# A two-layer trunk on one core: mixers' raw weight buffers at the other end of SBUF, FFN tiles in another order, ten unread products in the first projection

## The chip, the cores and the metric

One NeuronCore of one Trainium2 chip runs the whole program. The metric is device time in microseconds of one execution; the number given is the median of three. A profile is one execution recorded by the hardware profiler. TensorE is written PE, VectorE DVE, ScalarE ACT, GpSimd POOL and SyncE SP.

## What is computed

The input x is 512 tokens of 1024 values, fp32. Layer 0 mixes tokens with a gated MLP block and latent attention, layer 1 with retention; each mixer is followed by a SwiGLU FFN with 2816 hidden columns.

```python
def reference(x, ...):
    for l in range(2):
        h = rmsnorm(x, norm_mix[l])
        x = x + (even_mixer(h, ...) if l % 2 == 0 else odd_mixer(h, ...))
        h = rmsnorm(x, norm_ffn[l])
        x = x + swiglu(h, ffn_w_gate[l], ffn_w_up[l], ffn_w_down[l])
    return x

def swiglu(h, w_gate, w_up, w_down):
    return (jax.nn.silu(h @ w_gate) * (h @ w_up)) @ w_down
```

## The kernel before

**Products.** x lies transposed in SBUF as eight tiles of 128 features by 512 tokens. Every fp32 operand of a large product is split into a high and a low part (`split`, L281 to L283: ACT writes the high part, DVE the rest), and a product is three PE products (`mm3`, L288 to L290). `project` multiplies all eight h tiles by one or several weight tiles; `h_tiles` are written by `scaled_parts` (ACT L357, DVE L358).

**Weights.** All weights stand in one list in the order of their use, the tape. `Tape.load` takes the next entry: SP issues the DMA into a raw tile (L211), ACT casts the high part (L214), DVE makes the low part (L215). The parts have four slots, so an entry is cast when the entry four before it has been used up. `tape.ahead()` loads until four entries are ahead. A raw tile is written by the next load of its slot only after ACT and DVE have read it. Raw tiles come from a pool that each stage opens for itself: 3 tiles in the mixers (L429, L992), 7 in the FFNs (L823), 4 KB per partition each. Loads that the end of a stage issues ahead go into that stage's pool: the first four FFN entries lie in the mixer's raw tiles.

**FFN.** Pair 0 of column tiles is multiplied plainly (four entries, "whole"). The others go in pairs by a scheme with seven products in place of eight (L867): entries A11, A12 and A22 are loaded, S1 and S3 are sums of two blocks, for which SP loads the first and POOL adds the second by an accumulating DMA (L213), and S2 and S4 are added by DVE in place (L199). The h side needs sums too: `sums(k)` copies two x tiles to a `J` tile on ACT (L837), makes the four sums on DVE (L846 to L849, four operations) and splits them into `t_hi`, `t_lo`. The code has the first projection, then `ss.columns` (the norm's transposes, L318), `sums(0)`, `sums(1)`, the second projection, `sums(2)`, `sums(3)`, then the products. `finish` writes the activations to `a_hi0` to `a_hi7` and `a_lo0` to `a_lo7`, column tile m to number m % 8; `down` reads them in three parts, pairs 0 to 3, 4 to 7 and 8 to 10.

**Memory.** Pools that live throughout lie lowest. A stage opens its pools one above the other from the same base, in the order of the code, and closes them at its end. Before, each stage's raw pool is the first and so begins at the base. With `reuse_waits="tile"` a new tile waits for the readers and writers of those older tiles that lay at its own bytes, not for the whole pool. Above the base, in KB per partition, the FFN has raw 28, `fp` 64 (`t_hi`, `t_lo` 32, then `a` 32), `fp2` 20 (`J` 16, `t` 4). Layer 1's mixer has raw 12, `tmp` 16 (eight tiles `w`), then `od`: `cs` 4, `decay` 8, small ones, `R_turns`, the parts of q, k and v, attention weights, gates `g0` to `g3`, `Ro` and, last, `y0` to `y3`, the normed and gated head outputs that the output projection multiplies.

**Order.** The tile framework puts each engine's instructions into one queue, at compile time, and sets the waits. Instructions of one engine are not always in the order of the code. At run time an engine takes its queue in order.

**Start.** Twelve products of `ones` by `ones` into the bank `warm` (L276) precede the first projection; nothing reads that bank. x arrives in five chunks of 1, 1, 2, 2 and 2 tiles.

Of the kernel before, what the change touches and what calls it, by code (L numbers as in the profile page):

```python
# [11 lines left out]
F32R = mybir.dt.float32r  # L12
# [4 lines left out]
P = 128  # L17
# [129 lines left out]

CHUNK = 1024


HALF = 256
SHORT = 64
# [2 lines left out]
def turns(m, d):  # L155


    if m.shape[1] == 2 * d:
        return m.rearrange("p (j d) -> p d j", j=2)
    return m.rearrange("p (b j d) -> p b d j", j=2, d=d)  # L160
# [75 lines left out]
def trunk_kernel(ctx: ExitStack, tc: tile.TileContext, a: dict, out: bass.AP):  # L236
    nc = tc.nc
# [9 lines left out]
    def new_tmp(stack, bufs=2):  # L247
        env["tmp"] = stack.enter_context(tc.tile_pool(name="tmp", bufs=bufs, reuse_waits="tile"))
# [4 lines left out]
    def bank(name="bank"):  # L253
        return ps.tile([P, S], F32, name=name, tag="bank")

    tape = Tape(nc, parts, a["wtape"])

    def new_raw(stack, bufs):
        tape.raw = stack.enter_context(tc.tile_pool(name="raw", bufs=bufs, reuse_waits="tile"))

    gains = const.tile([P, 4, KD], F32, name="gains")
    nc.scalar.dma_start(out=gains, in_=a["gains"])
# [4 lines left out]
    ones = const.tile([P, P], F32, name="ones")  # L267
# [6 lines left out]
    warm = bank("warm")  # L274
# [6 lines left out]
    def split(dst_hi, dst_lo, src):  # L281
        nc.scalar.copy(dst_hi, src)  # L282
        nc.vector.tensor_tensor(dst_lo, src, f32(dst_hi), op=ALU.subtract)  # L283

    def mm3(acc, stat, mov, start, stop, d=HALF):

        (sh, sl), (mh, ml) = stat, [turns(m, d) for m in mov]
        nc.tensor.matmul(acc, sh, mh, start=start, stop=False)  # L288
        nc.tensor.matmul(acc, sh, ml, start=False, stop=False)  # L289
        nc.tensor.matmul(acc, sl, mh, start=False, stop=stop)  # L290
# [61 lines left out]
    def scaled_parts(which, k):  # L352


        hi, lo = h_tiles(k)
        g = gains[:, which, k : k + 1]
        nc.scalar.activation(hi, x[k], AF.Identity, scale=g)  # L357
        nc.vector.scalar_tensor_tensor(  # L358
            lo, x[k], g, f32(hi), op0=ALU.mult, op1=ALU.subtract
        )  # L360
        return hi, lo

    def project(h, n=1, name="ps_mm", d=HALF):

        w = [tape.next() for _ in range(n)]
        accs = [bank(name) for _ in range(n)]
        nk = w[0][0].shape[1]
        for k in range(nk):
            for (hi, lo), acc in zip(w, accs):
                mm3(acc, (hi[:, k, :], lo[:, k, :]), h[k], k == 0, k == nk - 1, d)  # L370
        tape.ahead()
        return accs[0] if n == 1 else accs

# [52 lines left out]


    with ExitStack() as e:
        new_raw(e, 3)  # L429
        h = []  # L430
        for k0, k1 in ((0, 1), (1, 2), (2, 4), (4, 6), (6, 8)):
            nc.sync.dma_start(out=x_all[:, k0:k1, :], in_=a["xP"][:, k0:k1, :])
# [45 lines left out]
            latp.append((hi, lo))  # L478

        kv_ss, q_ss = Norm(), Norm()  # L480
        accs = [project(h) for _ in range(3)]
        ss.columns(D)
        rcol = ss.kept_columns(ev)
        accs.append(project(h))
        R = ss.rows(norm)
        for acc in accs[:2]:
            kv_ss.add(latent(acc))
        q_ss.add(latent(accs[2]))
        q_ss.add(latent(accs[3]))
        q_ss.add(latent(project(h)))  # L490

        nc.vector.tensor_tensor(
# [37 lines left out]
        for i in range(NT):  # L530
# [4 lines left out]
                start=True,  # L535
                stop=True,
# [277 lines left out]
    def ffn(h, ss, which):  # L814
# [5 lines left out]


        with ExitStack() as e:
            new_raw(e, 7)  # L823
            fp = e.enter_context(tc.tile_pool(name="fp", bufs=1, reuse_waits="tile"))
            fp2 = e.enter_context(tc.tile_pool(name="fp2", bufs=2, reuse_waits="tile"))
            q = S // 2
            act = {}
            stands = {n: [] for n in ("A11", "A12", "S4", "S1", "S2", "S3", "A22")}
# [1 line left out]
            def wide():  # L830
                return fp2.tile([P, 2 * S], F32, name="J", bufs=4)

            def sums(k):

                f = wide()
                for j in range(2):
                    nc.scalar.activation(  # L837
                        f[:, j * S : (j + 1) * S],
                        x[2 * k + j],
                        AF.Identity,  # L840
                        scale=gains[:, which, 2 * k + j : 2 * k + j + 1],
                    )
                b11, b12, b21, b22 = (f[:, i * q : (i + 1) * q] for i in range(4))
                t = wide()
                t1, t2, t3, t4 = (t[:, i * q : (i + 1) * q] for i in range(4))
                nc.vector.tensor_tensor(t1, b11, b12, op=ALU.subtract)  # L846
                nc.vector.scalar_tensor_tensor(t2, t1, -1.0, b22, op0=ALU.mult, op1=ALU.subtract)
                nc.vector.tensor_tensor(t3, b22, b12, op=ALU.subtract)
                nc.vector.scalar_tensor_tensor(t4, t2, -1.0, b21, op0=ALU.mult, op1=ALU.subtract)  # L849
                hi = fp.tile([P, 4 * q], F32R, name=f"t_hi{k}")  # L850
                lo = fp.tile([P, 4 * q], F32R, name=f"t_lo{k}")
                split(hi, lo, t)
                for i, n in enumerate(("S1", "S2", "S3", "A22")):
                    stands[n].append([v[:, i * q : (i + 1) * q] for v in (hi, lo)])
                for n, j, i in (("A11", 0, 0), ("A12", 1, 0), ("S4", 1, 1)):
                    stands[n].append([v[:, i * q : (i + 1) * q] for v in h[2 * k + j]])
# [74 lines left out]
            for k in range(2):  # L931
                sums(k)
            whole.append(project(h, 2))
            for k in range(2, 4):
                sums(k)
# [45 lines left out]
    h = [scaled_parts(2, k) for k in range(KD)]  # L981
    h2 = []
    ss2 = None
    for k in ffn(h, ss, 2):
        ss2 = ss2 or Norm()
        h2.append(scaled_parts(1, k))
        ss2.add(x[k])
    h, ss = h2, ss2


    with ExitStack() as e:
        new_raw(e, 3)  # L992
        new_tmp(e)
        od = e.enter_context(tc.tile_pool(name="od", bufs=1, reuse_waits="tile"))
        cs = od.tile([P, 2, S], F32, name="cs")
# [5 lines left out]
        def parts_tile(name, n=S):  # L1001
            return (od.tile([P, n], F32R, name=name + "_hi"), od.tile([P, n], F32R, name=name + "_lo"))

        def rotated(name, accs):
            a1, a2 = (undone(acc) for acc in accs)
            c, s = plain(cs[:, 0, :]), plain(cs[:, 1, :])
            o = [tmp([P, S], "w", bufs=8), tmp([P, S], "w", bufs=8)]
            t = [tmp([P, S], "w", bufs=8), tmp([P, S], "w", bufs=8)]
            nc.vector.tensor_tensor(plain(o[0]), a1, c, op=ALU.mult)
            nc.vector.tensor_tensor(plain(t[1]), a1, s, op=ALU.mult)  # L1010
            nc.vector.tensor_tensor(plain(t[0]), a2, s, op=ALU.mult)
            nc.vector.tensor_tensor(plain(o[1]), a2, c, op=ALU.mult)
            nc.vector.tensor_tensor(o[0], o[0], t[0], op=ALU.subtract)
            nc.vector.tensor_tensor(o[1], o[1], t[1], op=ALU.add)
            got = []
            for j in range(2):
                p = parts_tile(f"{name}{j}")
                split(*p, o[j])
                got.append((*p, o[j]))
            return got  # L1020

        prev = None
        for hd in range(RH):
            accs = project(h, 2)
# [3 lines left out]
            else:  # L1028
                so.columns(512)
                q = rotated("q", accs)  # L1030
            accs2 = project(h, 2)
            if hd == 0:
# [5 lines left out]
                q = rotated("q", accs)  # L1038
            else:
                gated()  # L1040
            k = rotated("k", accs2)
            v = []
            for i, acc in enumerate(project_tokens(h, 4, 2)):
# [4 lines left out]
                hi, lo = parts_tile(f"v{i}")  # L1048
# [14 lines left out]
            for j in range(NT - 1):  # L1063
                n = S - j * P
# [62 lines left out]
    for m in ffn(h2, ss, 3):  # L1127
        nc.sync.dma_start(out=out[m * P : (m + 1) * P, :], in_=x[m])
# [69 lines left out]
```

## Time and profile before

| | |
|---|---|
| median of 3 runs | 1235.24 us (1233.83 to 1236.07) |
| the profiled execution | 1235.62 us |
| its span in the trace | 1233.8 us |
| PE busy | 1219.8 us, 99% |
| DVE, ACT, POOL busy | 853.1, 562.7, 83.7 us |
| granted clock over the span | 0.997 |

A busy time counts instructions as they lie in the trace; ends of products are modelled, so PE's busy time contains half-clock stretches and short waits. "Granted clock" is the share of PE's full clock in a stretch: 1.00 is 2.4 GHz, 0.50 is 1.2 GHz. In a timeline the columns are start, duration, engine, line, operation, tiles written and read, count, and in brackets the idle time of the engine before it with what ended it.

### The profile page before, as it was taken

The numbers are of one execution on the slowest core, as the hardware profiler recorded it, in microseconds if no ns is written. First come the engines' busy times: TensorE is split into PE (matmuls) and PEld (weight loads), VectorE is DVE, ScalarE is ACT, GpSimd is POOL, SyncE is SP. The second block draws the span as 40 slices with busy tenths as digits, with TensorE's granted clock in tenths as the row PEclk, the third lists the DMA queues.
The fourth block names the chain that finished last, engine by engine and source line by source line (L and its number), as shares of the span: only waits on it lengthen the run. The fifth ranks groups of instructions, "written<-read, shape, count | busy, mean of one in ns | idle before, by whom it ended". The sixth has DMA issues, their size and how long they took to land. (4 is left out here: it accounts for less than half of the span.)

```text
span 1233.8 us, 18406 instructions
## 1 busy us (share of the span) xinstructions
PE 1219.8 (99%) x7464; PEld 1105.8 (90%) x7464; DVE 853.1 (69%) x1224; ACT 562.7 (46%) x809; POOL 83.7 (7%) x84
## 2 busy tenths in 40 slices
PE   8999999999999999999999999999998999999998
PEld 7897778998999899888888888888888989998997
DVE  6597749875687577955574474574778756876774
ACT  5455747652465255533342242242465623652551
POOL 2072001000000000000000000000010000000000
PEclk9999999999999999999999999999999999999999
DMA  7223007555575466223122332332266555754631
GB/s 238 86 73 116 35 35 205 155 171 148 143 205 163 128 161 194 91 69 115 57 103 69 103 103 69 103 103 69 86 188 157 174 146 142 203 167 123 166 108 69
DMA packets 44772, 155.32 MB, mean 126 GB/s; under 512 B 5376, under 2 KB 5776, under 8 KB 44560
## 3 DMA queue, kind: packets, MB, share of 16 engines
q1 hardware_dynamic: 38304, 131.06, 31.8%
q0 software_dynamic: 6240, 23.08, 10.8%
q8 instruction: 58, 0.95, 0.3%
q14 instruction: 26, 0.21, 0.1%
q10 hardware_dynamic: 144, 0.02, 0.0%
HBM read 152.04 MB, written 2.10 MB: 125 GB/s over the span
## 5 line engine op out<-in xcount | busy, mean ns | idle before, releaser
L214 ACT CAST w_hi<-w_raw 128x1024 fp32r<-128x1024 f32 (+2 forms) x288 | 294.0, 1027 | 477.9 <-PE ps_mm L289 223.0
L215 DVE TENSOR_TENSOR w_lo<-w_raw,w_hi 128x1024 fp32r<-128x1024 f32 (+2 forms) x288 | 345.1, 1205 | 122.7 <-ACT w_hi L214 122.2
L288 PE MATMUL ps_mm<-h_hi,w_hi 128*128 128x512 f32 x456 | 175.6, 385 | 2.1 <-ACT h_hi L357 1.5
L289 PE MATMUL ps_mm<-h_lo,w_hi 128*128 128x512 f32 x456 | 173.8, 382 | 0.8 <-DVE h_lo L358 0.7
L290 PE MATMUL ps_mm<-h_hi,w_lo 128*128 128x512 f32 x456 | 173.5, 381 | 0.0
L867 PE MATMUL ps_x<-t_hi,w_hi 128*128 128x256 f32 x480 | 133.2, 278 | 4.1 <-ACT J L896 4.0
L288 PE MATMUL ps_mm<-a_hi,w_hi 128*128 128x512 f32 x352 | 133.3, 380 | 0.3 <-ACT a_hi L282 0.3
L289 PE MATMUL ps_mm<-a_lo,w_hi 128*128 128x512 f32 x352 | 133.4, 379 | 0.0
L290 PE MATMUL ps_mm<-a_hi,w_lo 128*128 128x512 f32 x352 | 133.4, 379 | 0.0
L867 PE MATMUL ps_x<-t_hi,w_lo 128*128 128x256 f32 x480 | 132.8, 277 | 0.0
L867 PE MATMUL ps_x<-t_lo,w_hi 128*128 128x256 f32 x480 | 132.7, 277 | 0.0
L288 PEld LDWEIGHTS ps_mm<-h_hi,w_hi 128*128 128x128 f32 x456 | 86.6, 190 | 15.7 <-ACT h_hi L357 2.2
L289 PEld LDWEIGHTS ps_mm<-h_lo,w_hi 128*128 128x128 f32 x456 | 86.6, 190 | 13.6 <-DVE h_lo L358 1.8
L290 PEld LDWEIGHTS ps_mm<-h_hi,w_lo 128*128 128x128 f32 x456 | 86.6, 190 | 12.7 <-DVE w_lo L215 0.4
L867 PEld LDWEIGHTS ps_x<-t_hi,w_hi 128*128 128x128 f32 x480 | 92.9, 194 | 5.3 <-ACT J L896 5.3
L867 PEld LDWEIGHTS ps_x<-t_lo,w_hi 128*128 128x128 f32 x480 | 92.9, 194 | 0.0
L867 PEld LDWEIGHTS ps_x<-t_hi,w_lo 128*128 128x128 f32 x480 | 92.9, 193 | 0.0
L213 POOL DMA_DIRECT2D w_raw<-in_wtape x40 | 34.8, 870 | 623.6 <-DVE t L881 159.2
L288 PEld LDWEIGHTS ps_mm<-a_hi,w_hi 128*128 128x128 f32 x352 | 66.4, 189 | 10.3 <-ACT a_hi L282 1.1
L290 PEld LDWEIGHTS ps_mm<-a_hi,w_lo 128*128 128x128 f32 x352 | 66.5, 189 | 9.4
L289 PEld LDWEIGHTS ps_mm<-a_lo,w_hi 128*128 128x128 f32 x352 | 66.6, 189 | 9.2
L925 DVE TENSOR_TENSOR t<-ps_mm,R 128x512 f32<-128x512 f32 x48 | 33.1, 689 | 58.8 <-PE ps_mm L290 58.6
(221 smaller groups left out, 2590.6 us busy)
## 6 DMA issues: line engine op xcount, KB each, us to landing
w_raw<-in_wtape SPq DMA_DIRECT2D x225, 512.0 KB, 3.4
w_raw<-in_wtape POOLq DMA_DIRECT2D x40, 512.0 KB, 6.1
w_raw<-in_wtape SPq DMA_DIRECT2D x19, 384.0 KB, 3.5
out_T<-x SPq DMA_DIRECT2D x8, 256.0 KB, 2.0
x<-in_xP SPq DMA_DIRECT2D x3, 512.0 KB, 7.5
w_raw<-in_wtape SPq DMA_DIRECT2D x4, 256.0 KB, 6.0
decay<-in_decay POOLq DMA_DIRECT2D x1, 1024.0 KB, 7.5
x<-in_xP SPq DMA_DIRECT2D x2, 256.0 KB, 3.6
```

The costliest lines, as they stand in the source:

```text
L213: nc.gpsimd.dma_start(out=t[:, c], in_=more[:, c], accum_op=ALU.add)
L214: nc.scalar.copy(hi[:, c], t[:, c])
L215: nc.vector.tensor_tensor(lo[:, c], t[:, c], hi[:, c].bitcast(F32), op=ALU.subtract)
L288: nc.tensor.matmul(acc, sh, mh, start=start, stop=False)
L289: nc.tensor.matmul(acc, sh, ml, start=False, stop=False)
L290: nc.tensor.matmul(acc, sl, mh, start=False, stop=stop)
L867: nc.tensor.matmul(o, s[:, k, cols], m, start=start and k + f + n == 0, stop=k == KD // 2 - 1 and n == 2, skip_group_check=True,)
L925: nc.vector.tensor_tensor(plain(t), undone(accs[j]), plain(R), op=ALU.mult)
```

## The change

The raw pools of the three stages get a side: `right` for the two mixers, which puts the pool at the upper end of SBUF and lets `tmp` and the pools after it move down by 12 KB, and `left` for the FFNs. The FFN's one pool `fp` is divided: `ft` (`t_hi`, `t_lo`) comes directly above the raw tiles, then `fp2` (`J`, `t`), then `fp` with the `a` tiles alone. The very first projection gets 6, 2, 1 and 1 products of `ones` by `ones` into `warm` in the code behind its first four chunks of products.

```diff
+IDLE = (6, 2, 1, 1)
-    def new_raw(stack, bufs):
-        tape.raw = stack.enter_context(tc.tile_pool(name="raw", bufs=bufs, reuse_waits="tile"))
+    def new_raw(stack, bufs, side):
+        tape.raw = stack.enter_context(tc.tile_pool(name="raw", bufs=bufs, side=side, reuse_waits="tile"))
-    def project(h, n=1, name="ps_mm", d=HALF):
+    def project(h, n=1, name="ps_mm", d=HALF, idle=()):
                 mm3(acc, (hi[:, k, :], lo[:, k, :]), h[k], k == 0, k == nk - 1, d)
+            for _ in range(idle[k] if k < len(idle) else 0):
+                nc.tensor.matmul(warm[:, :P], ones, ones, start=True, stop=True)
         tape.ahead()
-        new_raw(e, 3)
+        new_raw(e, 3, "right")
-        accs = [project(h) for _ in range(3)]
+        accs = [project(h, idle=IDLE), project(h), project(h)]
-            new_raw(e, 7)
+            new_raw(e, 7, "left")
+            ft = e.enter_context(tc.tile_pool(name="ft", bufs=1, reuse_waits="tile"))
+            fp2 = e.enter_context(tc.tile_pool(name="fp2", bufs=2, reuse_waits="tile"))
             fp = e.enter_context(tc.tile_pool(name="fp", bufs=1, reuse_waits="tile"))
-            fp2 = e.enter_context(tc.tile_pool(name="fp2", bufs=2, reuse_waits="tile"))
-                hi = fp.tile([P, 4 * q], F32R, name=f"t_hi{k}")
-                lo = fp.tile([P, 4 * q], F32R, name=f"t_lo{k}")
+                hi = ft.tile([P, 4 * q], F32R, name=f"t_hi{k}")
+                lo = ft.tile([P, 4 * q], F32R, name=f"t_lo{k}")
-        new_raw(e, 3)
+        new_raw(e, 3, "right")
```

## Rows read from the trace of the kernel before

**Rows 1.** The page, engine shares: busy time, share of the span, instructions.

```profile
PE 1219.8 (99%) x7464; PEld 1105.8 (90%) x7464; DVE 853.1 (69%) x1224; ACT 562.7 (46%) x809; POOL 83.7 (7%) x84
```

**Rows 2.** Waits of PE, whole span: what waited, for what, total us, times, longest.

```profile
PE ps_x L867 <- ACT J L896: 4.0, 2, 2.8
```

**Rows 3.** Windows: us, busy by engine (instructions), granted clock, DMA share, GB/s.

```profile
206.75:231.38 24.63, 24.63 (x178) 23.34 (x176) 23.48 (x32) 17.34 (x22) 2.92 (x3) 1.00 0.47 108
907.95:940.01 32.06, 27.32 (x178) 25.27 (x176) 24.35 (x33) 15.59 (x20) 4.61 (x5) 0.95 0.76 201
...
936.00:939.20 3.20, 3.20 (x17) 3.20 (x17) 3.00 (x4) 0.48 (x1) 0.00 (x0) 0.50 0.70 155
```

**Rows 4.** Timeline of ACT, layer 1's FFN start.

```profile
917.49 1.04 ACT L214 CAST w_hi<-w_raw 128x1024 fp32r<-128x1024 f32 x1 [6.50 <-DMA w_raw<-in_wtape]
```

**Rows 5.** POOL's first accumulating DMA there: timeline, and its landing.

```profile
908.42 0.93 POOL L213 DMA_DIRECT2D w_raw<-in_wtape  x1 [46.56 <-DVE J L849]
...
DMA to landing us min/median/max: 9.0/9.0/9.0
```

**Rows 6.** Timelines of SP and DVE ahead of it (a DMA row: issue time).

```profile
888.63 0.33 SPq L211 DMA_DIRECT2D w_raw<-in_wtape  x1
...
902.72 3.54 SPq L211 DMA_DIRECT2D w_raw<-in_wtape  x7
...
901.43 1.22 DVE L215 TENSOR_TENSOR w_lo<-w_raw,w_hi 128x1024 fp32r<-128x1024 f32 x1
```

**Rows 7.** Timelines at layer 0's FFN start: SP, POOL, ACT, DVE.

```profile
187.05 12.37 SPq L211 DMA_DIRECT2D w_raw<-in_wtape  x8
...
196.20 0.91 POOL L213 DMA_DIRECT2D w_raw<-in_wtape  x1 [95.08 <-PE ps_mm L290]
...
190.78 0.70 ACT L837 ACTIVATE J<-x,gains 128x512 f32<-128x512 f32 x1
...
202.90 0.42 DVE L846 TENSOR_TENSOR J<-J 128x256 f32<-128x256 f32 x1
```

**Rows 8.** Timelines of DVE, PE and ACT, layer 1, end of mixer.

```profile
869.92 3.19 DVE L1108 TENSOR_TENSOR w<-g,Ro 128x512 f32<-128x512 f32 x4
...
879.41 0.69 DVE L283 TENSOR_TENSOR y_lo<-w,y_hi 128x512 fp32r<-128x512 f32 x1
...
897.59 0.38 PE L288 MATMUL ps_mm<-h_hi,w_hi 128*128 128x512 f32 x1
...
898.52 0.72 ACT L837 ACTIVATE J<-x,gains 128x512 f32<-128x512 f32 x1
...
903.17 0.42 DVE L846 TENSOR_TENSOR J<-J 128x256 f32<-128x256 f32 x1
...
904.85 0.75 DVE L358 SCALAR_TENSOR_TENSOR h_lo<-x,gains,h_hi 128x512 fp32r<-128x512 f32 x1
```

**Rows 9.** Start of layer 1's mixer: PE, POOL, readers of `cs`.

```profile
520.30 0.38 PE L288 MATMUL ps_mm<-h_hi,w_hi 128*128 128x512 f32 x1
...
534.33 1.03 POOL L296 TENSOR_TENSOR rs_r<-rs_r,mhalf 128x4 f32<-128x4 f32 x1 [46.58 <-DVE rs_r L294]
...
L1037 DVE TENSOR_TENSOR cs<-cs,R x2: 677/680/684, 544.6 to 545.2; 128x512 f32<-128x512 f32 x2
```

**Rows 10.** The start: windows (first L276 alone), then timelines of PE and DVE.

```profile
4.20:5.50 1.30, 1.27 (x11) 1.08 (x10) 1.00 0.98 288
...
10.99:14.40 3.41, 3.41 (x9) 2.69 (x10) 3.41 (x6) 3.41 (x7) 0.00 (x0) 0.50 1.03 395
...
5.87 0.48 PE L288 MATMUL ps_mm<-h_hi,w_hi 128*128 128x512 f32 x1 [0.40 <-ACT w_hi L214]
...
10.09 0.48 PE L288 MATMUL ps_mm<-h_hi,w_hi 128*128 128x512 f32 x1 [1.52 <-ACT h_hi L357]
...
13.93 1.41 DVE L358 SCALAR_TENSOR_TENSOR h_lo<-x,gains,h_hi 128x512 fp32r<-128x512 f32 x2
...
16.33 0.38 PE L288 MATMUL ps_mm<-h_hi,w_hi 128*128 128x512 f32 x1
```

## Prediction

> **What bounds the kernel now.** I read the page's engine shares first, then TensorE's waits, then the stages in windows, and only then the queues that feed the one stage that stands out. The page has TensorE (PE) busy 99% of the span [rows 1]: a change gains only where PE stands still or runs at half clock, and loses only where it makes PE stand still. One wait of PE is long, 4.0 us in two waits for ACT's copy of a product [rows 2], and the windows say where. The two FFN layers run the same code. From the norm's transposes in the middle of the first four weight tiles to the first product of pair 2, 178 PE records each, layer 0 takes 24.63 us and layer 1 takes 32.06 us [rows 3]: **7.43 us** more. PE's busy time in layer 1's stretch is 27.32 us, so 4.74 are plain waiting; the rest is what follows a wait: from 936.0 to 939.2 the granted clock is 0.50 (1.2 GHz of 2.4) [rows 3].
>
> Why does layer 1 wait? PE waits for ACT and VectorE (DVE), and ACT had stood still before: 6.50 us to 917.49, for a weight tile's DMA [rows 4]. ACT and DVE work through their queues in order, so the FFN's operand sums (L837 to L849) and their splits sat behind this one tile, then came in a bunch too late. The tile is S1, the sum of two blocks: SP loads the first, GpSimd (POOL) adds the second by an accumulating DMA. POOL issued that at 908.42 and it took 9.0 us to land [rows 5]. It could not issue before SP's part had landed, and SP issued nothing between 888.96 and 902.72, then seven loads in 3.54 us [rows 6]. What held SP was the write of a raw buffer still being read: the split that reads the mixer's last raw tile is DVE's L215 at 901.43, 1.22 us long, ending at 902.65 [rows 6]. Today the FFN's raw pool begins at the address where the mixer's raw pool begins, so its first load waits for the mixer's last split. Layer 0 has the same overlap, but its loads went out from 187.05 on and POOL's sum was issued at 196.20 [rows 7], 10.6 us ahead of the norm's transposes at 206.75; layer 1's at 908.42 was 0.5 us behind them (907.95) [rows 3].
>
> **The change, part by part.**
>
> *Raw buffers at the right end.* In KB per partition above the base of the stage pools, worked out from the tile shapes: the FFN's seven raw tiles lie at 0 to 28. In the changed kernel layer 1's mixer has there its `w` temporaries (0 to 16), `cs` (16 to 20) and `decay` (20 to 28). The last reader of any of these is the split of the last head's output, DVE's `y_lo<-w` at 879.41, done at 880.10 [rows 8]. So A11's load can follow the load issued at 888.63, at about 889.0 instead of 902.72; S1's SP load at 889.4; POOL's sum comes 5.7 us after A11's load, as now (902.72 to 908.42), at 894.7, and lands 9.0 us later at 903.7. S1's cast cannot start before the first projection frees its slot at 907.95, so it has 4 us to spare. What is late next? By layer 0, nothing: there the same instructions fill 24.63 us of PE in 24.63 us [rows 3]. I take the whole **7.43 us**; the bounds are 0 (the tile comes no earlier) and 7.43.
>
> *Cost on the other side.* In layer 1's mixer the raw tiles now lie over the FFN's right end. Layer 0's mixer needs 103.1 KB beside them, so they start no lower than 103.1, and the FFN ends at 112: at most 8.9 KB overlap, the `a` tiles numbered 7 and 6, unused in the last `down`, and at most the end of number 4, which the last `down` product reads. A load over that one waits until 520.30 [rows 9]. It is a value chunk, due only after four projections of 24 products at 0.2158 us (48 products from 897.59 to 907.95 [rows 3, 8]), 20.7 us later; load, cast and split take under 8 us. Behind it in SP's queue stand only later loads. `cs` and `decay`, on POOL's queue, now lie over raw tiles of the last `down` and of the next mixer's keys, read by about 519; behind them POOL has the rsqrt at 534.33, and `cs` is first read at 544.6 [rows 9]. Both cost nothing; without that cover each microsecond beyond 12 would cost one.
>
> *FFN tiles in another order.* `J` moves from 92 to 60 KB. Today it lies over the last head's `y`, read by PE until 897.59, and ACT's first write to `J` comes at 898.52 [rows 8]. In the changed kernel it lies over attention weights and gates, last read when `w` is made, from 869.92 for 3.19 us [rows 8]. So ACT can copy x tiles into `J` during the output projection. In layer 0 `J` already comes early: ACT writes it at 190.78 while DVE's sums start at 202.90, behind the last h split [rows 7]. I book nothing for it beyond the 7.43 (bounds: the sums' place in DVE's queue, rival 3).
>
> *Ten unread products.* They need only `ones`, so what fills PE's queue may put them between the first tile's chunks or directly behind the twelve warming products: instructions do not keep the order of the code (DVE's sum L846 at 903.17 stands ahead of an h split at 904.85 that the code has before it [rows 8]). One costs 0.24 us at the rate from 4.2 to 5.5 us (11 half products in 1.3 us [rows 10]) and twice that at half clock: 2.4 to 4.7 us in all. From 5.87 on PE has the two first chunks' six products, 1.3 us, and then waits for h 2 until 10.09 [rows 10], so 2.9 us fit before 10.09 with no delay; at half clock throughout, 4.7 + 2.6 end at 13.2, 3.1 us late. What the ten can give back is the half clock from 10.99 to 14.40 [rows 10]. But the first tile's end does not follow the clock: its last h split ends on DVE at 15.34, and two products must follow, 15.8 at full clock, where today the next tile starts at 16.33 [rows 10]. So the gain is at most **0.5 us**, the loss at most 3.1. I take 0.5: before 10.09 PE is then busier than today by all ten products, and the rate from 4.2 to 5.5 shows that the clock was already full when they come.
>
> The Trainium skill (TensorE: Matmul & The Clock Gate, section Part 1: The HAM clock gate) says that half clock is the default and that activity releases it. By that alone the ten products would be worth half of the 3.41 us at 0.50, an estimate of 1.7 us, and the sum would be 1226.1. The trace's DVE row caps it at 0.5, so the sum does not use it.
>
> **The sum.** The profiled execution took 1235.62 us (span 1233.8, 1.8 around it). 1235.62 - 7.43 - 0.5 = 1227.7. It was 0.38 above the median of the three runs, 1235.24, so the forecast for the median is **1227.3 us**.
>
> **Rivals.**
> 1. *The sum tile stays late.* The accumulating DMA took 9.0 us [rows 5]. If it takes over 13 us when issued during the output projection, ACT waits again; half of the stall left gives 1231. Against it: when it took 9.0 it shared the engines with seven loads, and these run earlier too, with nothing else beside them. Chance 0.10. The Trainium skill (SBUF — State Buffer, section SBUF: two separate sides) has another reason for a slow POOL DMA: its descriptors wait while DVE holds a shared port. The trace leaves it open: in layer 0 DVE was busy 23.48 of 24.63 us [rows 3] and the tile was in time.
> 2. *The change does not do what it says.* The first FFN load still waits for something read late, and the ten products change no clock. Time 1234.7 to 1235.6. Against it: the overlap above leaves no late reader under the raw tiles. Chance 0.09.
> 3. *Slower: the sums overtake the h splits.* With `J` free early, DVE may take two sums (four operations, five of which fill the 1.68 us from 903.17 to 904.85 [rows 8], and a split of 1.2, so 2.5 each) ahead of the last h splits, at both FFN starts. In layer 1 the last split ends at 905.60 [rows 8] and is due at 897.59 + 42 x 0.2158 = 906.65, so 5.1 us of sums would cost 4.0; in layer 0 (done at 202.9 [rows 7], due 1.3 us ahead of 206.75) 2.5; each followed by a half-clock stretch as long as the 3.2 us seen [rows 3], 1.6. In all 9.7 us lost against 7.9 gained: 1237.0. It turns slower once the loss passes 7.9, which takes two sums at both places. Against it: layer 0's order, `J` written at 190.78 and summed at 202.90 [rows 7]. Chance 0.06.
> 4. *Something smaller given back*: one sum ahead in one place, or the ten products at half clock, 1 to 3 us: 1228.5 to 1230.5. Chance 0.13.
>
> **How the numbers follow.** The forecast has 0.62 (1226 to 1228.5: the runs of before spread by 1.4 below and 0.8 above their median), rival 4 has 0.13, rival 1 0.10, rival 2 0.09, rival 3 0.06. The range from 1225.8 to 1231.5 holds the forecast, rival 4 and half or more of rival 1, 0.81. A measurement of this kernel can tell about 0.2%, 2.5 us, from no change: faster is below 1232.8. Faster: 0.62 + 0.13 + 0.08 of rival 1 = 0.83; same: rival 2 and the rest of rival 1, 0.11; slower 0.06.
>
> **What would show it.** Right: SP's loads for layer 1's FFN begin at 889 without the pause; POOL's first sum is issued near 895; ACT has no wait on a weight DMA between the norm's transposes and pair 2; that window takes about 24.7 us at granted clock 1.00; the second weight tile starts near 15.8. Wrong: a pause of SP after the mixer's last load; PE waiting for h splits at either FFN start; a value chunk late near 541.

## The result, and the profile of the changed kernel

The changed kernel takes 1227.55 us (median of six, 1227.29 to 1228.05) where the kernel before takes 1235.2 (six, 1233.83 to 1236.07): a ratio of 0.9939, 95% interval 0.9926 to 0.9952. The profiled execution took 1227.61 us, its span is 1225.8, its mean granted clock 0.999. The forecast was 1227.3. Line numbers of the changed kernel lie a little higher: L213 and L215 are the loads (before L211 and L213), L216 and L217 cast and split of weights, L290 to L292 the three products, L320 the norm's transposes, L359 and L360 the h splits, L375 the unread products.

First the page's engine shares and all waits of PE over the span (what waited, for what, total us, times, longest). The kernel before has, beside the 4.0 us for `ps_x` of [rows 2], this wait for a split of DVE:

```profile
PE ps_v L867 <- DVE t_lo L283: 0.7, 2, 0.4
```

In the changed kernel both are gone:

```profile
PE 1218.2 (99%) x7484; PEld 1105.6 (90%) x7484; DVE 852.8 (70%) x1224; ACT 563.2 (46%) x809; POOL 85.8 (7%) x84
...
PE warm L278 <- DVE mhalf L272: 1.1, 1, 1.1
PE ps_mm L290 <- ACT h_hi L359: 0.4, 1, 0.4
PE ps_mm L291 <- DVE h_lo L360: 0.3, 1, 0.3
PE ps_mm L290 <- ACT a_hi L284: 0.3, 2, 0.2
PE ps_mm L290 <- ACT qkT L709: 0.2, 1, 0.2
```

Then the two stretches of [rows 3], from the norm's transposes to the first product of pair 2 (us, busy by engine, granted clock, DMA share, GB/s):

```profile
206.18:230.83 24.65, 24.65 (x178) 23.35 (x177) 23.51 (x32) 17.39 (x22) 2.05 (x2) 1.00 0.32 87
907.38:932.06 24.68, 24.68 (x178) 23.39 (x177) 23.79 (x33) 15.94 (x20) 4.75 (x3) 1.00 0.47 109
```

Layer 1 now takes 24.68 us in place of 32.06, against layer 0's 24.65, at granted clock 1.00 and with PE busy throughout. That is 7.38 of the 8.0 us by which the span fell. The second weight tile of the program starts 0.54 earlier (below); 0.08 is spread over the rest.

The queues that feed layer 1's FFN start, as in [rows 4 to 6]: timelines of SP (issue time of DMAs), POOL and ACT, and the landing of POOL's first sum.

```profile
888.07 3.69 SPq L213 DMA_DIRECT2D w_raw<-in_wtape  x8
...
896.07 0.93 POOL L215 DMA_DIRECT2D w_raw<-in_wtape  x1 [34.77 <-DMA w_raw<-in_wtape]
...
907.15 0.85 POOL L215 DMA_DIRECT2D w_raw<-in_wtape  x1 [7.51 <-DVE J L853]
...
907.20 1.98 ACT L216 CAST w_hi<-w_raw 128x1024 fp32r<-128x1024 f32 x2
...
DMA to landing us min/median/max: 9.6/9.6/9.6
```

SP issues eight loads in 3.69 us from 888.07, the mixer's last one and the FFN's seven, with no pause. POOL's first sum goes out at 896.07, not at 908.42, and lands at 905.64. ACT casts A11 and S1 back to back from 907.20, with no idle time in brackets; before, S1's cast stood 6.50 us for its DMA.

The start, to be read beside [rows 10]:

```profile
8.96 0.61 PE L375 MATMUL warm<-ones 128*128 128x128 f32 x4
...
9.95 0.48 PE L290 MATMUL ps_mm<-h_hi,w_hi 128*128 128x512 f32 x1 [0.38 <-ACT h_hi L359]
...
15.79 0.38 PE L290 MATMUL ps_mm<-h_hi,w_hi 128*128 128x512 f32 x1
...
9.18 1.33 ACT L359 ACTIVATE h_hi<-x,gains 128x512 fp32r<-128x512 f32 x2 [1.27 <-DMA x<-in_xP]
...
13.79 1.41 DVE L360 SCALAR_TENSOR_TENSOR h_lo<-x,gains,h_hi 128x512 fp32r<-128x512 f32 x2
...
10.00:15.00 5.00, 4.45 (x19) 3.07 (x20) 5.00 (x8) 5.00 (x10) 0.00 (x0) 1.00 1.00 380
```

The unread products stand between the real ones (a product is two instructions in a row's count), PE's wait ahead of h 2 fell from 1.52 to 0.38 us, and the granted clock from 10 to 15 is 1.00. The second weight tile starts at 15.79 in place of 16.33. The end follows the h splits: PE still waits 0.3 us for one (`h_lo` above), DVE ends the last split at 13.79 + 1.41 = 15.20, and 0.59 later the tile is done.

### The profile page after: what moved, and what is told of

Read it like the earlier page. It is cut to its first block, busy times and chain, and to the rows that moved or that the text cites. A ratio compares the mean times of both kernels' runs of the same rounds, so it can differ in the third digit from the quotient of the medians.

```text
span 1225.8 us, 18440 instructions
## 1 busy us (share of the span) xinstructions
PE 1218.2 (99%) x7484; PEld 1105.6 (90%) x7484; DVE 852.8 (70%) x1224; ACT 563.2 (46%) x809; POOL 85.8 (7%) x84
## 5 line engine op out<-in xcount | busy, mean ns | idle before, releaser
L216 ACT CAST w_hi<-w_raw 128x1024 fp32r<-128x1024 f32 (+2 forms) x288 | 294.1, 1027 | 471.7 <-PE ps_mm L291 225.2
L217 DVE TENSOR_TENSOR w_lo<-w_raw,w_hi 128x1024 fp32r<-128x1024 f32 (+2 forms) x288 | 344.8, 1205 | 115.4 <-ACT w_hi L216 114.8
L290 PE MATMUL ps_mm<-h_hi,w_hi 128*128 128x512 f32 x456 | 175.1, 384 | 0.7 <-ACT h_hi L359 0.4
L292 PE MATMUL ps_mm<-h_hi,w_lo 128*128 128x512 f32 x456 | 172.8, 379 | 0.0
L290 PE MATMUL ps_mm<-a_hi,w_hi 128*128 128x512 f32 x352 | 133.3, 380 | 0.3 <-ACT a_hi L284 0.3
L292 PE MATMUL ps_mm<-a_hi,w_lo 128*128 128x512 f32 x352 | 133.4, 379 | 0.0
L290 PEld LDWEIGHTS ps_mm<-h_hi,w_hi 128*128 128x128 f32 x456 | 86.2, 189 | 13.5 <-ACT h_hi L359 0.6
L292 PEld LDWEIGHTS ps_mm<-h_hi,w_lo 128*128 128x128 f32 x456 | 86.2, 189 | 12.0
L215 POOL DMA_DIRECT2D w_raw<-in_wtape x40 | 34.7, 868 | 597.7 <-DMA w_raw<-in_wtape 283.4
L290 PEld LDWEIGHTS ps_mm<-a_hi,w_hi 128*128 128x128 f32 x352 | 66.4, 189 | 10.3 <-ACT a_hi L284 1.1
L292 PEld LDWEIGHTS ps_mm<-a_hi,w_lo 128*128 128x128 f32 x352 | 66.5, 189 | 9.4
```

The source lines that it names most:

```text
L215: nc.gpsimd.dma_start(out=t[:, c], in_=more[:, c], accum_op=ALU.add)
L216: nc.scalar.copy(hi[:, c], t[:, c])
L217: nc.vector.tensor_tensor(lo[:, c], t[:, c], hi[:, c].bitcast(F32), op=ALU.subtract)
```

## The experiments

The kernels are edits of the kernel before, unless the text says "of the changed kernel". Each ratio is to runs of the kernel before on the same chip. The first four kernels ran on one chip; S1 and S3 from one block and the first two kernels with the squares behind on a second; sides in layer 1's mixer only and the three kernels at the end on a third.

### One part of the change at a time

**Ten products alone.**

```diff
+IDLE = (6, 2, 1, 1)
-        accs = [project(h) for _ in range(3)]
+        accs = [project(h, idle=IDLE), project(h), project(h)]
```

> The kernel before with only the ten unread products added; nothing of the pools is moved. My account: the first weight tile's end follows the last h split on DVE, so the second tile starts at 15.8 in place of 16.33, granted clock 1.00 from 10 to 16, and the time falls by 0.5 us to 1234.7; layer 1's FFN start keeps its 32.06 us. Rival (the half clock is worth its own length): the second tile starts near 14.6 and the time falls by 1.7 us to 1233.5. Rival (the products delay the first chunk): the second tile starts after 16.33.

1234.85 us (ten, 1232.73 to 1235.79) against 1234.95 for the kernel before (19, 1233.1 to 1235.84): ratio 0.9998 [0.9988, 1.0007]. The times can't tell it from nothing. The profile can tell what it does: the granted clock from 10 to 15 is 1.00, as in the changed kernel, the second weight tile starts at 15.65 (forecast 15.8), and layer 1's waits for `ps_x`, 4.0 us, are all there.

**Sides alone.**

```diff
-        new_raw(e, 3)
+        new_raw(e, 3, "right")
```

(in both mixers, with `side` handed to the pool; the FFNs take "left")

> Only the sides of the raw pools: mixers' raw tiles on the right, the FFN's pools in the old order (J at 92 to 108 KB, over the last y tiles and over the mixer's raw tiles on the right). My account: the raw tiles alone carry the gain, so the window from the norm's transposes to pair 2 in layer 1 shrinks from 32.06 to about 24.7 and the time falls by 7.4 us to 1227.8, though J is written no earlier than 898.5. Rival (J carries it, or the overlap of J and t with the mixer's raw tiles costs): the window stays over 28 us and the time falls by less than 4.

1227.23 us (four, 1226.45 to 1227.62), ratio 0.9935 [0.992, 0.995]: the whole gain. SP has no pause, POOL's first sum goes out at 895.31, and layer 1's window takes 24.63 us as forecast (24.7):

```profile
888.08 4.16 SPq L211 DMA_DIRECT2D w_raw<-in_wtape  x8
...
895.31 0.93 POOL L213 DMA_DIRECT2D w_raw<-in_wtape  x1 [33.99 <-DMA w_raw<-in_wtape]
...
907.40:932.03 24.63, 24.63 (x177) 23.34 (x176) 24.05 (x32) 16.46 (x21) 3.66 (x2) 1.00 0.36 94
```

**Order alone.** The pool `ft`, then `fp2`, then `fp`, as in the change; sides and products as before.

> Only the FFN's pools in the other order, all raw pools on the left as before. My account: SP still pauses until 902.7 after the mixer's last load, the S1 tile still lands near 917, so the time falls by 0 to 2 us (the operand sums can be made earlier and fewer of them stand behind the late cast). Rival (J under y was what held the sums): the window shrinks to under 27 us and the time falls by over 5 us.

1235.0 us (ten, 1234.2 to 1235.39), ratio 1.0 [0.9991, 1.001]. SP's pause is there as before, seven loads from 902.16:

```profile
902.16 3.24 SPq L211 DMA_DIRECT2D w_raw<-in_wtape  x7
...
10.00:15.00 5.00, 5.00 (x15) 3.74 (x16) 5.00 (x8) 5.00 (x10) 0.00 (x0) 0.66 1.01 383
```

**Sides and order, without the ten products.**

> Both moves of pools, without the ten products. My account: layer 1's window about 24.7, the second weight tile at the start still at 16.33 after a half-clock stretch, time 1228.1, 0.5 us over the changed kernel. Rival (the products are worth 1.7 us): 1229.3.

1227.75 us (four, 1227.71 to 1228.08), ratio 0.9941 [0.9926, 0.9955]. That is 0.2 above the changed kernel, not the 0.5 expected, and on another chip; the second weight tile starts at 15.94, not at 16.33, because x came earlier. From the start of the second weight tile to the end of the span it takes 1210.06 us (1226.0 - 15.94), the changed kernel 1210.01, but sides alone 1209.62 (1225.8 - 16.18); the spans are rounded to 0.1. The 0.4 lies in one place, PE's rows at layer 0's FFN start, first sides alone, then sides and order:

```profile
199.73 0.38 PE L288 MATMUL ps_mm<-h_hi,w_hi 128*128 128x512 f32 x1
199.94 0.38 PE L289 MATMUL ps_mm<-h_lo,w_hi 128*128 128x512 f32 x1
```

```profile
199.49 0.38 PE L288 MATMUL ps_mm<-h_hi,w_hi 128*128 128x512 f32 x1
199.98 0.48 PE L289 MATMUL ps_mm<-h_lo,w_hi 128*128 128x512 f32 x1
```

With both, the second product starts 0.49 behind the first in place of 0.21: it waits for DVE, whose queue has the same splits and squares in another order. The kernel before has this wait too. So sides alone removed a small wait that the new order of the FFN tiles brings back; in whole times the two can't be told apart.

**Sides, in layer 1's mixer only.**

```diff
-        new_raw(e, 3)          # layer 1's mixer
+        new_raw(e, 3, "right")
```

> Sides alone, and only in layer 1's mixer: the raw pool of layer 0's mixer stays at the base. Theory (only the FFN start of layer 1 was late; layer 0's loads came early for nothing): the whole gain remains, 1227.3, with SP's loads out of 888 to 892 without a pause in layer 1 and the old ones, from 187 on, in layer 0. Rival (layer 0's earlier loads, or its mixer's raw tiles out of the way, carry part of it): 1228.5 or more.

1227.79 us (four, 1227.43 to 1228.46), ratio 0.9942 [0.9928, 0.9955]. SP's loads for layer 0's FFN go out as before [rows 7], those for layer 1's without the pause:

```profile
186.41 12.37 SPq L211 DMA_DIRECT2D w_raw<-in_wtape  x8
...
887.99 3.78 SPq L211 DMA_DIRECT2D w_raw<-in_wtape  x8
```

The gain is that of this one boundary. In layer 0 the earlier loads (POOL's first sum at 180.25 in the changed kernel, at 196.20 before) bring nothing that shows in whole times.

### Which tile, and why its sum is slow

**S1 from its first block alone**, in the kernel before.

```diff
-            for more in src[1:]:
+            for more in src[1:] if key != (1, 1, "S1") else ():
```

> The kernel before, in which S1 of pair 1 in layer 1 is loaded from its first block alone: POOL's accumulating DMA at 908.42 is left out, so that this one sum lacks its second block. SP's pause until 902.7 and the raw buffers' places stay. Theory (one late tile holds ACT's queue, and all the loss hangs on it): the tile is in SBUF with SP's load at about 907.8, ACT casts it at 908.7 with no wait, the window from the norm's transposes to pair 2 takes about 24.7 us in place of 32.06, and the time is about 7.4 below the kernel before, 1227.6. Rival (the burst behind SP's pause makes more than one tile late, S3's among them): the wait moves on to the next tile, the window stays above 28 us, the time above 1231.

1227.54 us (four, 1227.43 to 1227.61) against 1234.52 (15): ratio 0.9944 [0.993, 0.9958]. In whole times that is 7.0 less, where 7.4 was expected. SP's seven loads still go out at 902.01 only, yet ACT casts two tiles in a row at 907.06 and the window takes 24.63 us:

```profile
902.01 3.77 SPq L211 DMA_DIRECT2D w_raw<-in_wtape  x7
...
907.06 1.98 ACT L214 CAST w_hi<-w_raw 128x1024 fp32r<-128x1024 f32 x2
...
907.24:931.87 24.63, 24.63 (x177) 23.34 (x176) 23.74 (x33) 15.96 (x20) 5.84 (x4) 1.00 0.80 221
```

One accumulating DMA of the 40 on POOL's queue carries the whole difference of the window, 32.06 to 24.63 us. SP's pause costs nothing except through this sum; the raw buffers stay where they were.

**S3 from its first block alone**, the next sum in the same queue.

```diff
-            for more in src[1:]:
+            for more in src[1:] if key != (1, 1, "S3") else ():
```

> The kernel before, in which S3 of pair 1 in layer 1 is loaded from its first block alone: the accumulating DMA at 910.93 is left out, so that this sum lacks its second block. S1's sum stays, issued at about 908.4. It tells what makes S1's sum take 9.0 us. If it shares with the second sum on POOL's queue, it takes about 5.5 us alone, as the third sum did (917.79 to 923.24), lands at 914, ACT's wait is 3.5 us shorter, and the time is 2.5 to 3.5 below the kernel before, 1231.5 to 1232.5. If it shares with SP's burst of loads, it takes 9.0 again and the time is that of before, 1235. If S3 were the tile that matters and not S1, the time would fall to about 1227.6.

1234.5 us (ten, 1232.8 to 1235.56), ratio 0.9998 [0.9989, 1.0007]: no change. S1's sum, now alone in POOL's queue, still takes 8.9 us, and ACT still waits 6.25:

```profile
908.00 0.93 POOL L213 DMA_DIRECT2D w_raw<-in_wtape  x1 [46.40 <-DVE J L848]
...
916.96 1.04 ACT L214 CAST w_hi<-w_raw 128x1024 fp32r<-128x1024 f32 x1 [6.25 <-DMA w_raw<-in_wtape]
...
DMA to landing us min/median/max: 8.9/8.9/8.9
```

So it does not share with the second sum. That it shares with SP's burst of loads fits these sums: 9.0, 9.6 and 8.9 us when it went out with five of SP's loads in flight; in the changed kernel the third sum, issued at 907.15 when SP's last load (landed 906.59) was done, took 5.2. Over the profiles of all fourteen kernels, the 13 sums that went out with five of SP's loads in flight took 8.9 to 9.9 us, and the 503 that went out with none or one took 4.9 to 8.5, by the median 5.85. No run took the burst away alone, so this is argued, not shown.

### What ends the first weight tile

**The squares behind the splits**, in the changed kernel. The norm's squares of x tiles 2 to 7 (L312 on ACT, L313 on DVE) are queued behind the last h split of each engine.

```diff
         for k in range(KD):
-            ss.add(x[k])
+            with tc.issue_after(newest[0]) if k > 1 else ExitStack(), tc.issue_after(newest[1]) if k > 1 else ExitStack():
+                ss.add(x[k])
```

> The changed kernel, in which the norm's squares of x tiles 2 to 7 (ACT's Square and DVE's addition) stand behind the last h split on both engines; before, three of each stood among the splits. Theory (DVE's and ACT's chain of splits ends the first weight tile): with x's chunks landing at 9.15, 10.44 and 11.74, ACT ends the last h_hi at 13.1, DVE the last h_lo at 13.8, and the second weight tile starts 0.6 later, at 14.4 in place of 15.79; the time is 1226.1, 1.4 below the changed kernel. Rival (the weight tile's own cast and split, or x's arrival, is next, or the squares come too late for the norm's transposes at 26): the second tile starts at 15.0 or later, or PE waits near 25, and the time stays within 0.5 of the changed kernel, 1227.1 to 1227.6.

1226.56 us (five, 1225.97 to 1226.61), ratio to the kernel before 0.9935 [0.9922, 0.9949]. ACT writes six h tiles in a row, DVE splits four in a row, and the second weight tile starts at 14.41:

```profile
8.70 3.91 ACT L362 ACTIVATE h_hi<-x,gains 128x512 fp32r<-128x512 f32 x6 [0.93 <-DMA x<-in_xP]
...
11.08 2.73 DVE L363 SCALAR_TENSOR_TENSOR h_lo<-x,gains,h_hi 128x512 fp32r<-128x512 f32 x4
...
14.41 0.38 PE L290 MATMUL ps_mm<-h_hi,w_hi 128*128 128x512 f32 x1
...
10.00:15.00 5.00, 4.92 (x24) 3.76 (x23) 5.00 (x10) 5.00 (x10) 0.00 (x0) 1.00 1.01 384
```

The start is 1.38 earlier, but 0.48 of that is x: its third chunk was there at 8.70, in the changed kernel's profile at 9.18. Counted from there, the tile takes 5.71 us against 6.61, so the edit is worth **0.90**, not the 1.4 forecast. That 14.41 meets the forecast of 14.4 is luck. The expectation has three squares among the splits; behind x's third chunk DVE had two there (L313 at 11.26 and 13.19 in the changed kernel, 0.60 each), and a reduction (L512 at 10.79, 0.29) has slipped in. The end still follows the last split, 13.81, by 0.60.

**The same without the ten products** (and without the new order).

> Sides alone (no order, no ten products) with the same squares behind the splits. If the splits end at 13.8 as above, PE's half clock is no longer hidden behind them: eight products at half clock cost 8 x 0.21 = 1.7 us, of which the waits for the splits cover about 0.5, so the second tile starts at about 15.2 to 15.6 and the time is 0.8 to 1.2 above the same kernel with the ten products: 1226.9 to 1227.3. If the ten products do nothing here, the two are equal within 0.2.

1226.52 us (five, 1226.36 to 1227.62), ratio 0.9939 [0.9926, 0.9951]. By the medians the ten products would seem to do nothing, 1226.52 beside 1226.56. But this kernel lacks the new order too, which costs 0.4 behind the start (from the second weight tile to the end it takes 1209.6 us, the kernel with order and products 1210.1). And its five executions are of two kinds: three have a granted clock of 1.000 over the span and take 1226.36 to 1226.52, two have 0.998 and take 1227.29 and 1227.62. The profiled one is of these: PE waits 1.44 us for h 2, and from 10 to 15 the clock is 0.66. Its second weight tile starts at 16.17, later than the 15.2 to 15.6 expected, but x's third chunk was late too (9.52): the tile takes 6.65 us from there, against 5.71, so the half clock costs 0.94, within the 0.8 to 1.2 expected.

```profile
10.30 0.76 PE L288 MATMUL ps_mm<-h_hi,w_hi 128*128 128x512 f32 x1 [1.44 <-ACT h_hi L360]
...
10.00:15.00 5.00, 4.68 (x13) 3.50 (x14) 4.72 (x8) 5.00 (x10) 0.00 (x0) 0.66 1.01 385
```

**Three kernels on one chip**: the changed kernel; the squares behind the splits; and that one with the ten products in the warming loop.

> The changed kernel itself, beside the next two on one chip, so that they are compared on it and not across chips. 1227.5, about 7.6 below the kernel before; second weight tile at about 6.6 us behind the landing of x's third chunk.

> The changed kernel with the squares behind the splits, as above, now beside the changed kernel on one chip. If the chain of splits was what ended the first weight tile, 0.9 below the changed kernel (5.73 us from the landing of x's third chunk to the second weight tile, against 6.64), 1226.6 where that has 1227.5. If the lower time above was the chip's, the two are equal within 0.3.

```diff
-IDLE = (6, 2, 1, 1)
+IDLE = ()
-    for _ in range(12):
+    for _ in range(22):
```

> The squares behind the splits, and the ten unread products in the warming loop (22 there, none among the chunks). If what matters is that PE has work between the chunks, ahead of h 2, the half clock comes back in many executions as without the ten products: a granted clock near 0.66 from 10 to 15 in those, and a median or an upper end about 1.0 above the kernel with the products among the chunks, 1227.5. If it matters only that ten more products run before the first real one, the clock stays 1.00 there and the time equals that kernel's, 1226.5, or is up to 0.2 below, since PE's 24 products then have no unread ones among them.

| five executions each | median, us | from, to |
|---|---|---|
| kernel before (9) | 1235.02 | 1232.85, 1236.3 |
| changed | 1227.35 | 1227.17, 1227.82 |
| squares behind | 1226.61 | 1226.16, 1227.27 |
| squares behind, ten in front | 1226.28 | 1226.19, 1227.12 |

The chain of splits is confirmed: the squares behind take 0.74 off (0.9 was expected), with 5.70 us from x's third chunk (8.73) to the second weight tile (14.43), against 6.61 in the changed kernel (8.70 and 15.31). With the ten in front PE's first real product starts at 8.82, but the second weight tile again 5.70 behind x (9.56 and 15.26), the clock is 1.00 from 10 to 15, and over the span it is 1.000 in all five executions:

```profile
8.82 0.46 PE L290 MATMUL ps_mm<-h_hi,w_hi 128*128 128x512 f32 x1
...
10.00:15.00 5.00, 4.66 (x19) 2.89 (x18) 4.68 (x8) 5.00 (x10) 0.00 (x0) 1.00 0.97 368
```

So the place among the chunks was not needed in these five executions. But this run does not part the two readings that were set against each other: products in front push the real ones back, and PE has no long idle time ahead of h 2 in either kernel. What both have in common is just that. The last row is the lowest median of all, 0.9930 [0.9918, 0.9943] of the kernel before and 1.07 us below the changed one; from the row above it the executions do not part it. With sides alone in place of sides and order it might save the 0.4 above as well; that wasn't tried.

## Why the prediction was right, step by step

**The late tile: right, and shown.** The steps were: raw buffers apart, SP at 889 without a pause, POOL's sum near 894.7, landing near 903.7, no wait of ACT, a window of about 24.7 us, 7.43 gained. Measured: 888.45 for the first FFN load, no pause, 896.07, 905.64, no wait, 24.68 us, 7.38. Sides alone give the gain, and leaving out the one accumulating DMA gives it without them.

**The size of the margin: off.** The sum was taken to go out 5.7 us behind A11's load; it took 7.6 (888.45 to 896.07), since S1's own SP load took 6.6 us to land (888.92 to 895.53) where it had taken 4.7 (903.10 to 907.77). The mixer's last load, issued at 888.07, was still in flight with it, which may be why; no run tests it. Then the sum took 9.6 us, not 9.0. ACT began S1's cast at 907.20 + 0.95 = 908.15, so 2.5 us were to spare, not 4. The time is unharmed, as the cast waits for its slot anyway; but rival 1 was nearer than its 0.10 said. What was held against it ("nothing else beside them") was wrong: SP's burst moved along with the sum, and five of its loads were in flight when the sum went out.

**The new order: nothing, for another reason.** The forecast had ACT copy x into `J` during the output projection. ACT's first write comes at 897.96, before at 898.52 [rows 8], just the 0.56 by which this whole stretch is earlier: `J` was not what held it. DVE's queue in layer 1 also has the same five sum operations ahead of the last h split as before (the split at 904.28, before at 904.85 [rows 8]). Rival 3 did not come about, not because DVE was quick enough, but because the order did not change there. In layer 0 the order is not neutral beside sides alone: it has the wait of 0.3 to 0.4 us that sides alone removes, which the forecast did not have.

**The other side of memory: nothing, as forecast.** PE's waits over the whole span list no value chunk, `cs` or `decay`.

**The ten products: right size in this profile, less on the average.** The second weight tile started at 15.79 (forecast 15.8), at full clock, and the last split capped it. That the number fits so well is luck, as the working behind it was off in two places that cancel: the last split ended at 15.20 and not 15.34, because x came 0.13 earlier, and 0.59 follow it, not 0.43. So of the 0.54 gained, 0.41 are the products' and 0.13 are x's. The profiles of ten kernels (from ACT's first h of x's third chunk to the second weight tile) show more:

| squares among the splits | us |
|---|---|
| with the ten products: changed, changed again, ten alone | 6.61, 6.61, 6.61 |
| without: before, sides alone, sides and order, S3 from one block | 7.02, 7.02, 7.02, 7.03 |
| without: order alone, S1 from one block, layer 1's side only | 6.63, 6.69, 6.63 |

All seven without the products have the half clock (0.66 to 0.67 from 10 to 15). In four it lasts until 14.2 to 14.5 and costs 0.41; in three it is over by 13.3 to 13.4, and DVE's chain hides it to within 0.08. The products are thus worth 0.4 in some executions and next to nothing in others, below what whole times can tell. With the chain shortened, the half clock costs 0.94 us where it falls, in two of five executions without the products. How often it falls with them is less sure. A half clock of 3.4 us, as in [rows 10], takes 0.0014 off the clock over the span, so 1.000 rules it out, but 0.999 does not: the profiles of sides alone and of sides and order have 0.999 with it. With the ten in front all five executions have 1.000; with the ten among the chunks and the squares behind, three of ten have 1.000 and the rest 0.999, and neither of the two profiles has it.

The Trainium skill (TensorE: Matmul & The Clock Gate, section Part 1: The HAM clock gate) has PE's activity release the half clock. The rows agree: 0.66 to 0.67 from 10 to 15 in all profiles without the products, 1.00 in all with them. But three executions of the kernel above without them had 1.000 over the span, so the products do not decide alone. The 1.7 us estimated from that rule did not come, since a chain on two other engines ended 0.6 us before the tile did.

The Trainium skill (SBUF — State Buffer, section SBUF: two separate sides) lets POOL's DMA descriptors wait while DVE, in some of its instructions, holds a port that both use. No run here tests that by itself, but the windows of two sums speak against DVE's load as the reason, first S1's in the kernel before, then the third in the changed one (DVE's busy time is the fourth number):

```profile
908.42:917.41 8.99, 8.99 (x44) 7.89 (x43) 3.87 (x7) 2.56 (x4) 2.83 (x3) 1.00 1.03 304
907.15:912.39 5.24, 5.24 (x28) 4.58 (x27) 5.24 (x9) 4.21 (x6) 0.85 (x1) 1.00 0.63 102
```

DVE was busy for 3.87 of the 8.99 us of the slow sum and for all 5.24 us of the quick one. What each of its instructions held, the trace does not show.

## What to carry to other kernels

Where two stages run the same code and one takes longer, measure the same stretch in both: the difference is the prize, and the wait that only one has leads back to its cause, here through ACT's queue to one DMA, one buffer address and one late reader. Before a buffer is placed, ask who reads last what lay at its bytes: a load issued ahead of its stage is ahead only if the tile beneath it is dead by then. Work that only keeps the clock up gave here no more than the next chain left, so look for that chain first; moving six squares behind six splits gave 0.9 us where the products gave at most 0.4.

## What the runs showed of the hardware that was not expected

- The landing of x's third chunk moved between 8.7 and 9.6 us from one profiled execution to another (ACT's first h of it: 8.70, 9.04, 9.18, 9.31, 9.56), and the whole program moves with it. From the second weight tile to the end the spread is far smaller: 1210.0 to 1210.1 us in eight profiles of kernels that have the gain (sides alone is at 1209.6, with and without the squares behind). The two profiles of the changed kernel differ by 0.4 us in the span, 1225.8 and 1225.4, and by 0.48 in x's landing.
- The half-clock stretch in the start came in some executions of one and the same kernel (squares behind, no ten products) and not in others: 0.998 against 1.000 over the span, 0.8 to 1.3 us apart, part of it x's landing. The kernel before varies likewise: of its 15 executions on the second chip, seven have 0.997 (median 1235.2 us), seven 0.998 (1233.6) and one 1.000 (1233.4). The profile that the forecast was taken from has 0.997, with a half-clock stretch at the start and one in layer 1's FFN, so the gain in a single execution depends on which it is compared with.
- An accumulating DMA of 512 KB took 8.9 to 9.9 us where it went out with five plain loads in flight (13 cases) and 5.0 to 6.6 us where none was in flight from its issue to its landing (18 cases), and leaving out the other accumulating DMA next to it changed nothing (8.9).
